# A recurrence's job order, one bias product, one tile's index scores and a closing norm

## The chip, the cores and the metric

One core of a Trainium2 chip runs the whole program in one launch. The metric is the time of an execution on the device in microseconds.

## The reference

Two blocks in a row over 512 tokens of 1024 features. The first has a gated recurrence (RG-LRU) layer and an attention layer that selects its keys, each with an MLP behind it; the second a gated linear attention with a pooling branch and a gated feed-forward layer; a norm closes. The change touches the recurrence, the index scores and the closing norm:

```python
def rglru_mixer(h, w_in, conv_w, conv_b, w_a, b_a, w_x, b_x, lam, w_out):
    gate, xr = jnp.split(h @ w_in, 2, axis=-1)
    gate = jax.nn.gelu(gate)
    xc = conv_b + sum(xpad[:, k:k + S] * conv_w[k] for k in range(4))
    r = sigmoid(blockwise(xc, w_a) + b_a)      # 4 blocks of 256 features
    i = sigmoid(blockwise(xc, w_x) + b_x)
    log_a = -8.0 * r * softplus(-lam)
    a, u = exp(log_a), sqrt(-expm1(2.0 * log_a)) * (i * xc)
    hs = scan(h_t = a_t * h_(t-1) + u_t)
    return (hs * gate) @ w_out

# attention, per block of 128 queries: 8 index heads choose the keys
dots = relu(einsum('bqhd,bsd->bqhs', qi_b, ki))
score = einsum('bqh,bqhs->bqs', wi_b, dots)
_, idx = lax.top_k(where(causal, score, -inf), topk)
logits = einsum('bqhc,bqkc->bqhk', q_lat_b, c_sel) + rel_bias[t5_bucket(dist)]

# at the very end
out = x * rsqrt(mean(x * x, axis=-1) + 1e-6) * norm_final
```

## The kernel before

Activations are kept transposed, as tiles of 128 features by 512 tokens. A matrix product takes its fp32 operands as a high and a low part and sums three matmuls, high by high, high by low and low by high (L349 to L351 in `group`); `lin` (L353) makes one output tile of 1024 inputs with 24 of them. There are eight PSUM banks.

Weights come as chunks of 128x1024 in the order of a table that `weight_plan` (L100) writes. `Weights` (L218) loads a chunk by SP (L246), makes its high part on ACT (L252) and its low part on DVE, or on POOL for the attention's inputs and a few others (L253); buffers of the high and low parts are reused in turn, so a copy waits until PE has left an earlier chunk.

Work is written as jobs, lists of stages. `run` (L269) interleaves them: at each step the next job's first stage, then later stages of the jobs before it. A scheduler of the framework sets the final order on each engine from that, and `tc.high_priority` brings some evictions forward.

In the recurrence `conv_job(j)` makes tile j of `xr` (PE), scales it (DVE, L536), and applies the convolution, one instruction on ACT (L541) and three taps on DVE (L544); `split` copies the high part on ACT (L362) and subtracts the low part on DVE (L363). `recur_job(b)`, called ax below, multiplies two such tiles by the two gates' weights: 24 matmuls into four banks. Tanh on ACT (L568, L569) frees these banks; then exponentials, a square root and factors follow, and a scan on DVE (L598). `rgate_job(j)` makes tile j of `gate`, with a gelu on ACT (L612) and the product with the scan's result on DVE (L615), and splits it: Y. `bias_job` loads two small tables, multiplies them (L635), copies the result on DVE (L639) and stores it to DRAM (L640) for attention. `rout` (L655) is the output product: its first four tiles take all of Y in pairs of tiles.

The order there is written by the loop at L645: xr0 to xr5, ax0, xr6, xr7, ax1, gates 0 and 1, ax2, bias job, gates 2 and 3, ax3, gates 4 to 7.

`index_job(i, h)` (L769) makes the scores of query block i and index head h: two matmuls into a bank (L779), relu with a scale on ACT (L784), then the weighted add into `score`, by ACT for head 0 (L790) and by DVE for the others (L793); for block 3 POOL does three heads. `select` (L802) then takes the largest keys in 16 rounds of two DVE instructions (L811, L812).

The end: `last_job` makes the last down products, four tiles of all tokens, then four tiles of the left 256 tokens, then of the right; each adds to x (L1453), squares (L1427, L1429) and prepares `fin`. `norm_job` (L1460) sums the squares over features with a matrix of ones (L1467), takes the root (L1471) and reciprocal (L1472) of the 128x256 result, in which all 128 rows are alike, multiplies four `fin` tiles (L1477) and stores them (L1478). The left half's norm is put between the right half's jobs.

Of the kernel before, what the change touches and what calls it, by code (L numbers as in the profile page):

```python
# [15 lines left out]
AF = mybir.ActivationFunctionType  # L16
# [80 lines left out]
    return plan  # L97


def weight_plan():  # L100

    plan = []
    for step in range(8):
        plan += [("xr" if step < 4 else "rgate", 2 * step % 8 + i) for i in range(2)]
        if 2 <= step <= 5:
            plan += [("ax", step - 2)]
    plan += [("routk", kk) for kk in range(4)] + [("rout", j) for j in range(4, 8)]
    plan += mlp_plan(0, HID_GROUPS, False)
    plan += [("att", j) for j in (0, 1, 2, 3, 4, 6, 7, 8, 9, 5, 10, 11, 12, 13)] + [("uk",), ("uv",)]
    plan += [("wo", j) for j in range(8)]  # L110
    plan += mlp_plan(1, HID_GROUPS, False)
    plan += [("lr",), ("k", 0), ("k", 1), ("k", 2), ("dec",), ("k", 3)] + [("q", j) for j in range(4)]
    plan += [("u", j) for j in range(4)] + [("v", half, kk) for half in range(2) for kk in range(4)] + [("pg",)]
    plan += [("gb", j) for j in range(8)]
    plan += [("ga", j) for j in range(4)] + [("r", j) for j in range(8)] + [("ga", j) for j in range(4, 8)]
    plan += [("bg", j) for j in range(8)] + [("wo2", j) for j in range(8)]
    plan += mlp_plan(0, HID2_GROUPS, True)
    return plan
# [150 lines left out]
def run(jobs):  # L269

    deep = max(len(j) for j in jobs)
    for step in range(len(jobs) + deep - 1):
        for stage in [0] + list(range(deep - 1, 0, -1)):
            i = step - stage
            if 0 <= i < len(jobs) and stage < len(jobs[i]):
                jobs[i][stage]()
# [3 lines left out]
def build(ctx, tc, xT, wall, par, relb, onehot, edges, out):  # L280
# [12 lines left out]
    def T(dt=F32, name="t"):  # L293
        return tp.tile([P, S], dt, name=name, tag="t")
# [117 lines left out]
    def residual_job(j, mm, feed, half=False):  # L412
        st = {}

        def first():
            st["ps"] = mm()

        def second():
            if half:
                stt(xs[j], st["ps"], 0.5, xs[j], op0=ALU.mult, op1=ALU.add)  # L420
            else:
                V.tensor_add(xs[j], xs[j], st["ps"])  # L422
            if feed is not None:
                feed.add(xs[j])

        return [first, second]
# [124 lines left out]
    def recur_job(b):  # L551
        st = {}

        def mm():
            h, l = W.get("ax", b)
            for nt in range(2):
                for m in range(2):
                    ps = st[nt, m] = PS()
                    o = m * 512 + nt * P
                    group(ps, [(h[:, o + k * 256:o + k * 256 + P], l[:, o + k * 256:o + k * 256 + P], *xcs[2 * b + k])  # L560
                               for k in range(2)])

        def gates():
            for nt in range(2):
                j = 2 * b + nt
                rg, ig = T(name="rg"), T(name="ig")
                with tc.high_priority(offset=EARLY):
                    act(rg, st[nt, 0], AF.Tanh, scale=0.5, bias=hb[:, j:j + 1])  # L568
                    act(ig, st[nt, 1], AF.Tanh, scale=0.5, bias=hb[:, KD + j:KD + j + 1])  # L569
                st[nt] = rg, ig  # L570
            for nt in range(2):
                j = 2 * b + nt
                rg, ig = st[nt]
                q = T(name="q")
                act(q, rg, AF.Exp, scale=nsp[:, j:j + 1], bias=nsp[:, j:j + 1])
                act(q, q, AF.Identity, scale=0.5, bias=half_t)
                act(rg, rg, AF.Tanh, scale=nsp2[:, j:j + 1], bias=nsp2[:, j:j + 1])
                st[nt] = rg, ig, q

        def factors():  # L580
            for nt in range(2):
                rg, ig, q = st[nt]
                stt(ig, ig, 1.0, xc[2 * b + nt], op0=ALU.add, op1=ALU.mult)
                w = T(name="w")
                stt(w, rg, 1.0, q, op0=ALU.subtract, op1=ALU.mult)
                stt(q, w, 2.0, q, op0=ALU.add, op1=ALU.mult)
                V.tensor_mul(ig, ig, q)
            for nt in range(2):
                rg, ig, q = st[nt]
                act(rg, rg, AF.Sqrt, scale=-1.0)  # L590

        def scan():
            for nt in range(2):
                rg, ig, q = st[nt]
                V.tensor_mul(ig, ig, rg)
                act(q, q, AF.Identity, scale=2.0, bias=minus_t)
                hh = hs[2 * b + nt] = T(name="hs")
                V.tensor_tensor_scan(hh, q, ig, 0.0, op0=ALU.mult, op1=ALU.add)  # L598

        return [mm, gates, factors, lambda: None, scan]  # L600
# [24 lines left out]
    def bias_job():  # L625
        st = {}

        def load():
            st["rb"], st["oh"] = T(name="relb"), T(name="oh")
            nc.sync.dma_start(st["rb"][:32, :P], relb)  # L630
            nc.sync.dma_start(st["oh"][:32, :DIST_PITCH], onehot)

        def mm():
            st["ps"] = PS("bias")
            PE.matmul(st["ps"][:, :DIST_PITCH], st["rb"][:32, :P], st["oh"][:32, :DIST_PITCH], start=True, stop=True)  # L635

        def store():
            t = T(name="biasrow")
            V.tensor_copy(t[:16, :DIST_PITCH], st["ps"][:16, :DIST_PITCH])  # L639
            nc.sync.dma_start(bdram, t[:16, :DIST_PITCH])  # L640

        return [load, lambda: None, mm, store]

    jobs = [[lambda: None, softplus]]
    for step in range(8):  # L645
        jobs += [(conv_job if step < 4 else rgate_job)(2 * step % 8 + i) for i in range(2)]
        if 2 <= step <= 5:
            jobs.append(recur_job(step - 2))
        if step == 4:
            jobs.append(bias_job())  # L650
    run(jobs)
    nxt = Feed("g_mlp0")
    rout_ps = []
# [14 lines left out]
                        PE.matmul(rout_ps[i], l[:, c], yh, start=False, stop=kt == KD - 1)  # L668
        return rout_ps[j] if j < 4 else lin(Y, "rout", j)

    run([residual_job(j, lambda j=j: rout(j), nxt) for j in range(KD)])
    feed, nxt = nxt, Feed("g_mix1")
    mlp(0, feed, nxt)

# [95 lines left out]
    def index_job(i, h):  # L770

        st = {}
        w = (i + 1) * P
        on_pool = i == 3 and h in (2, 4, 6)

        def mm():
            ps = st["ps"] = PS("idx")
            for n in range(2):
                PE.matmul(ps[:, :w], qi[h][:, i * P:(i + 1) * P], ki[n][:, :w], start=n == 0, stop=n == 1)  # L779

        def relu():

            d = st["d"] = T(name="dots") if on_pool else st["ps"]
            act(d[:, :w], st["ps"][:, :w], AF.Relu, scale=wis[i][0][:, h:h + 1])  # L784

        def add():
            d, sg = st["d"], wis[i][1][:, h:h + 1]
            if h == 0:
                accs[i] = T(name="score")
                act(accs[i][:, :w], d[:, :w], AF.Copy, scale=sg)  # L790
            else:
                if not on_pool:
                    stt(accs[i][:, :w], d[:, :w], sg, accs[i][:, :w], op0=ALU.mult, op1=ALU.add)  # L793
                else:
                    G.tensor_scalar(d[:, :w], d[:, :w], sg, 1.0, op0=ALU.mult, op1=ALU.mult)
                    G.tensor_add(accs[i][:, :w], accs[i][:, :w], d[:, :w])
            if h == 7:
                V.tensor_add(accs[i][:, w - P:w], accs[i][:, w - P:w], tri)
                ready[i] = True

        return [mm, relu, add]
# [658 lines left out]
    def norm_job(c):  # L1460
        st = {}
        w = c.stop - c.start

        def tot():
            ps = st["ps"] = PS("tot")[:, :w]
            for i in range(2):
                PE.matmul(ps, ones, acc2[i][:, c], start=i == 0, stop=i == 1)  # L1467

        def rstd():
            r = st["r"] = T(name="std")[:, :w]  # L1470
            act(r, st["ps"], AF.Sqrt, scale=1.0 / D, bias=eps_t)  # L1471
            V.reciprocal(r, r)  # L1472

        def outs(pairs):
            for i in pairs:
                z = fin[i, c.start].rearrange("p (d c) -> p d c", d=2)
                V.tensor_mul(z, z, st["r"].unsqueeze(1).to_broadcast([P, 2, w]))  # L1477
                nc.sync.dma_start(out[2 * i:2 * i + 2, :, c].rearrange("d p c -> p d c"), z)  # L1478

        return [tot, rstd, lambda: outs((1, 0)), lambda: outs((2, 3))]  # L1480
# [30 lines left out]
    jobs += [last_job(d, left, first, n, hid) for d in range(KD - 4, KD)]  # L1511
    jobs += [last_job(d, right, first, n, hid) for d in range(KD - 4, KD)]
    norm_left, norm_right = norm_job(left), norm_job(right)
    jobs.insert(-2, norm_left[:3])
    run(jobs)
    norm_right[0]()
    norm_left[3]()
# [32 lines left out]
```

## Time and profile before

| | us |
|---|---|
| median of 3 runs | 1905.28 |
| the runs | 1903.79, 1905.28, 1905.71 |
| profiled execution | 1903.61 |
| its span, first to last instruction | 1901.8 |
| PE, DVE, ACT, POOL busy | 1848.7, 1020.3, 813.4, 181.7 |

Mean granted clock of PE over the span is 0.988 of full speed. Times of the trace count from the start of the span.

### The profile page before, as it was taken

How to read it: one execution, taken by the hardware profiler on the slowest of the kernel's cores; microseconds unless marked ns; L12 is line 12 of the kernel's file. 1: busy time of each engine (PE TensorE's matmuls, PEld its weight loads, DVE VectorE, ACT ScalarE, POOL GpSimd, SP SyncE). 2: the span in 40 equal slices, each digit the busy share in tenths (PEclk: the TensorE clock that was granted, in tenths of full speed). 3: DMA queues.
4: the chain of work that ended last, by engine and by line, in shares of the span. 5: the costliest groups of instructions: out<-in, count | busy, mean ns of one | idle time of the engine just before them, and what ended most of it. 6: DMA issues, size and time to landing. Idle time of an engine off the chain costs nothing.

```text
span 1901.8 us, 21845 instructions
## 1 busy us (share of the span) xinstructions
PE 1848.7 (97%) x8434; PEld 1526.0 (80%) x8434; DVE 1020.3 (54%) x1512; ACT 813.4 (43%) x1271; POOL 181.7 (10%) x194
## 2 busy tenths in 40 slices
PE   8989999999999679999999999999999999999997
PEld 6868888888878468888888888888888888888886
DVE  7886543344349956654244445735584554344345
ACT  6784432333244577443234445446543333132223
POOL 0000000000155264000000014211000000000000
PEclk9999999999999899999999999999999999999998
DMA  5222222222222530322222222231122222222221
GB/s 197 84 86 92 100 98 91 100 100 96 93 100 90 146 89 21 111 93 96 100 100 92 97 100 86 92 111 45 67 89 100 100 89 100 100 95 94 100 80 53
DMA packets 61000, 179.36 MB, mean 94 GB/s; under 512 B 7696, under 2 KB 18144, under 8 KB 60896
## 3 DMA queue, kind: packets, MB, share of 16 engines
q1 hardware_dynamic: 60752, 177.97, 27.6%
q8 instruction: 66, 1.08, 0.2%
q14 instruction: 38, 0.31, 0.0%
q10 hardware_dynamic: 144, 0.00, 0.0%
HBM read 168.48 MB, written 2.12 MB: 90 GB/s over the span
## 4 chain that ended last, share of the span: by engine, by line
PE 63%; DVE 4%; ACT 2%; issue 1%; DMA 0%; POOL 0%; SPq 0%; DVEq 0%; ACTq 0%
PE ps L349 14%; PE ps L351 13%; PE ps L350 13%; PE dn L350 5%; PE dn L351 5%; PE dn L349 5%; PE o L1319 1%; DVE score L812 1%; PE v L1225 1%; PE v L1224 1%; PE v L1226 1%; DVE top L811 1%; ACT probs L941 1%; PE kv L1293 1%; PE tot L376 0%
## 5 line engine op out<-in xcount | busy, mean ns | idle before, releaser
L252 ACT ACTIVATE wh<-wst 128x1024 fp32r<-128x1024 f32 (+2 forms) x314 | 328.2, 1047 | 910.3 <-PE ps L350 358.7
L349 PE MATMUL ps<-xh,wh 128*128 128x512 f32 x1376 | 542.5, 394 | 6.4 <-DVE biasrow L639 4.6
L351 PE MATMUL ps<-xh,wl 128*128 128x512 f32 x1376 | 536.6, 390 | 0.0
L350 PE MATMUL ps<-xl,wh 128*128 128x512 f32 x1376 | 536.5, 390 | 0.0
L253 DVE TENSOR_TENSOR wl<-wst,wh 128x1024 fp32r<-128x1024 f32 (+2 forms) x291 | 352.4, 1212 | 224.3 <-ACT wh L252 197.2
L349 PEld LDWEIGHTS ps<-xh,wh 128*128 128x128 f32 x1376 | 259.3, 188 | 62.8 <-issue 7.2
L350 PEld LDWEIGHTS ps<-xl,wh 128*128 128x128 f32 x1376 | 259.3, 188 | 56.3 <-issue 2.4
L351 PEld LDWEIGHTS ps<-xh,wl 128*128 128x128 f32 x1376 | 259.1, 188 | 54.1
L349 PE MATMUL dn<-h,wh 128*128 128x512 f32 (+1 forms) x712 | 271.7, 382 | 0.0
L350 PE MATMUL dn<-l,wh 128*128 128x512 f32 (+1 forms) x712 | 271.7, 382 | 0.0
L351 PE MATMUL dn<-h,wl 128*128 128x512 f32 (+1 forms) x712 | 271.7, 382 | 0.0
L350 PEld LDWEIGHTS dn<-l,wh 128*128 128x128 f32 x712 | 133.8, 188 | 26.0
L349 PEld LDWEIGHTS dn<-h,wh 128*128 128x128 f32 x712 | 133.8, 188 | 26.0
L351 PEld LDWEIGHTS dn<-h,wl 128*128 128x128 f32 x712 | 133.8, 188 | 25.8
L253 POOL TENSOR_TENSOR wl<-wst,wh 128x1024 fp32r<-128x1024 f32 x23 | 55.2, 2405 | 934.7 <-ACT wh L252 934.5
L422 DVE TENSOR_TENSOR x<-x,dn 128x512 f32<-128x512 f32 x48 | 33.0, 687 | 170.8 <-PE dn L351 170.8
L453 DVE SCALAR_TENSOR_TENSOR relu<-ps,std 128x512 f32<-128x512 f32 x64 | 44.2, 691 | 146.7 <-PE ps L351 146.6
L349 PE MATMUL ps<-h,wh 128*128 128x512 f32 x200 | 78.7, 396 | 5.5 <-ACT h L362 3.5
L350 PE MATMUL ps<-l,wh 128*128 128x512 f32 x200 | 77.8, 389 | 0.0
L351 PE MATMUL ps<-h,wl 128*128 128x512 f32 x200 | 77.8, 389 | 0.0
L349 PEld LDWEIGHTS ps<-h,wh 128*128 128x128 f32 x200 | 37.9, 190 | 15.1 <-ACT h L362 4.0
L1497 DVE TENSOR_TENSOR u<-ps,std 128x512 f32<-128x512 f32 x22 | 15.2, 690 | 62.5 <-PE ps L351 62.5
(315 smaller groups left out, 2129.2 us busy)
## 6 DMA issues: line engine op xcount, KB each, us to landing
wst<-wall SPq DMA_DIRECT2D x300, 512.0 KB, 3.2
btile<-biasdram SPq DMA_DIRECT2D x32, 128.0 KB, 3.0
qd<-qq SPq DMA_DIRECT2D x64, 64.0 KB, 2.1
wst<-wall SPq DMA_DIRECT2D x8, 384.0 KB, 3.0
x<-xT SPq DMA_DIRECT2D x8, 256.0 KB, 4.9
out_dram<-fin SPq DMA_DIRECT2D x8, 256.0 KB, 2.3
wst<-wall SPq DMA_DIRECT2D x6, 256.0 KB, 5.0
kto<-kth SPq DMA_DIRECT2D x8, 128.0 KB, 2.7
```

What stands on the lines that cost most here:

```text
L252: self.nc.scalar.activation(h[:, a:b], st[:, a:b], AF.Copy)
L253: eng.tensor_sub(l[:, a:b], st[:, a:b], h[:, a:b].bitcast(F32))
L349: PE.matmul(ps, wh, xh, start=i == 0, stop=False)
L350: PE.matmul(ps, wh, xl, start=False, stop=False)
L351: PE.matmul(ps, wl, xh, start=False, stop=i == n - 1)
L422: V.tensor_add(xs[j], xs[j], st["ps"])
L453: stt(t, st["ps"], 0.0, feed.r, op0=ALU.max, op1=ALU.mult)
L811: V.max(top, acc[:, :w])
L812: V.match_replace(acc[:, :w], top, acc[:, :w], MARK)
L941: act(s[:, :w], s[:, :w], AF.Exp, scale=-1.0, bias=nm, accum_out=sums[:, a:a + 1])
L1224: PE.matmul(st["ps"][i], xh, hk, start=kt == 0, stop=False)
L1225: PE.matmul(st["ps"][i], xh, lk, start=False, stop=False)
```

## The change

1. The order of the recurrence's jobs becomes a table, LAYER0, that sets jobs and weights alike: xr0 to xr6, ax0, xr7, gate 0, ax1, gates 1 and 2, ax2, gates 3 and 4, ax3, gates 5 to 7.
2. The bias job leaves the recurrence and runs between the fourth and the fifth job of the output product.
3. For query block 1, relu writes its result to a tile in SBUF, not back into its bank. The other blocks stay.
4. The closing norm sums squares with x's columns as weights and a single column of ones, so that 256 tokens become 128x2 numbers with tokens on partitions; root and reciprocal work on 128x2; two products with the identity bring the result back to all rows of 128x256, in a bank that the outputs read. The left half's norm is put one job earlier.

```diff
--- before.py
+++ after.py
@@ -97,13 +97,14 @@
     return plan
 
 
+
+LAYER0 = ([("xr", j) for j in range(7)] + [("ax", 0), ("xr", 7), ("rgate", 0), ("ax", 1), ("rgate", 1), ("rgate", 2)]
+          + [("ax", 2), ("rgate", 3), ("rgate", 4), ("ax", 3)] + [("rgate", j) for j in range(5, 8)])
+
+
 def weight_plan():
 
-    plan = []
-    for step in range(8):
-        plan += [("xr" if step < 4 else "rgate", 2 * step % 8 + i) for i in range(2)]
-        if 2 <= step <= 5:
-            plan += [("ax", step - 2)]
+    plan = list(LAYER0)
     plan += [("routk", kk) for kk in range(4)] + [("rout", j) for j in range(4, 8)]
     plan += mlp_plan(0, HID_GROUPS, False)
     plan += [("att", j) for j in (0, 1, 2, 3, 4, 6, 7, 8, 9, 5, 10, 11, 12, 13)] + [("uk",), ("uv",)]
@@ -642,12 +643,7 @@
         return [load, lambda: None, mm, store]
 
     jobs = [[lambda: None, softplus]]
-    for step in range(8):
-        jobs += [(conv_job if step < 4 else rgate_job)(2 * step % 8 + i) for i in range(2)]
-        if 2 <= step <= 5:
-            jobs.append(recur_job(step - 2))
-        if step == 4:
-            jobs.append(bias_job())
+    jobs += [{"xr": conv_job, "ax": recur_job, "rgate": rgate_job}[n](j) for n, j in LAYER0]
     run(jobs)
     nxt = Feed("g_mlp0")
     rout_ps = []
@@ -668,7 +664,8 @@
                         PE.matmul(rout_ps[i], l[:, c], yh, start=False, stop=kt == KD - 1)
         return rout_ps[j] if j < 4 else lin(Y, "rout", j)
 
-    run([residual_job(j, lambda j=j: rout(j), nxt) for j in range(KD)])
+    jobs = [residual_job(j, lambda j=j: rout(j), nxt) for j in range(KD)]
+    run(jobs[:4] + [bias_job()] + jobs[4:])
     feed, nxt = nxt, Feed("g_mix1")
     mlp(0, feed, nxt)
 
@@ -780,7 +777,7 @@
 
         def relu():
 
-            d = st["d"] = T(name="dots") if on_pool else st["ps"]
+            d = st["d"] = T(name="dots") if on_pool or i == 1 else st["ps"]
             act(d[:, :w], st["ps"][:, :w], AF.Relu, scale=wis[i][0][:, h:h + 1])
 
         def add():
@@ -1462,14 +1459,20 @@
         w = c.stop - c.start
 
         def tot():
-            ps = st["ps"] = PS("tot")[:, :w]
-            for i in range(2):
-                PE.matmul(ps, ones, acc2[i][:, c], start=i == 0, stop=i == 1)
+
+            ps = st["ps"] = PS("tot")
+            for n in range(w // P):
+                cols = slice(c.start + n * P, c.start + (n + 1) * P)
+                for i in range(2):
+                    PE.matmul(ps[:, n:n + 1], acc2[i][:, cols], ones[:, 0:1], start=i == 0, stop=i == 1)
 
         def rstd():
-            r = st["r"] = T(name="std")[:, :w]
-            act(r, st["ps"], AF.Sqrt, scale=1.0 / D, bias=eps_t)
-            V.reciprocal(r, r)
+            col = small(w // P, "rstd")
+            act(col, st["ps"][:, :w // P], AF.Sqrt, scale=1.0 / D, bias=eps_t)
+            V.reciprocal(col, col)
+            st["r"] = PS("r")[:, :w]
+            for n in range(w // P):
+                PE.matmul(st["r"][:, n * P:(n + 1) * P], col[:, n:n + 1].to_broadcast([P, P]), ident, start=True, stop=True)
 
         def outs(pairs):
             for i in pairs:
@@ -1511,7 +1514,7 @@
     jobs += [last_job(d, left, first, n, hid) for d in range(KD - 4, KD)]
     jobs += [last_job(d, right, first, n, hid) for d in range(KD - 4, KD)]
     norm_left, norm_right = norm_job(left), norm_job(right)
-    jobs.insert(-2, norm_left[:3])
+    jobs.insert(-3, norm_left[:3])
     run(jobs)
     norm_right[0]()
     norm_left[3]()
```

In these rows the numbers behind a tile's name tell apart the tiles of one name. PE, at ax0 (h_460 is the high part of the first convolution's tile, xh the layer's input). Before:

```order
L349 MATMUL ps_435<-xh_188,wh_308 128x512
L350 MATMUL ps_435<-xl_189,wh_308 128x512
L351 MATMUL ps_435<-xh_188,wl_309 128x512
L349 MATMUL ps_485<-h_460,wh_340 128x512
L349 MATMUL ps_492<-h_460,wh_340 128x512
L349 MATMUL ps_499<-h_460,wh_340 128x512
```

PE, the end of xr6 and what follows it, now:

```order
L351 MATMUL ps_485<-xl_183,wh_340 128x512
L352 MATMUL ps_485<-xh_182,wl_341 128x512
L350 MATMUL ps_485<-xh_188,wh_340 128x512
L351 MATMUL ps_485<-xl_189,wh_340 128x512
L352 MATMUL ps_485<-xh_188,wl_341 128x512
L350 MATMUL ps_527<-h_460,wh_382 128x512
L350 MATMUL ps_534<-h_460,wh_382 128x512
```

The 24 matmuls of xr6 (ps_485, the last of them shown) now stand ahead of ax0's first ones, which stood right behind xr5 (ps_435).

ACT, ahead of the second ax job's first tanh. Before (h_709 is the high part of xr6's convolution, whose taps are xc_663; xc_713 is xr7's):

```order
L541 ACTIVATE xc_663<-xr_627,params_74 128x512
L252 ACTIVATE wh_735<-wst_734 128x1024
L596 ACTIVATE q_576<-q_576,minus_115 128x512
L362 ACTIVATE h_709<-xc_663 128x512
L541 ACTIVATE xc_713<-xr_668,params_74 128x512
L568 ACT_TABLE_LOAD
L568 ACTIVATE rg_718<-ps_635,half_b_218 128x512
L569 ACTIVATE ig_719<-ps_642,half_b_218 128x512
```

ACT, ahead of the second ax job's first tanh, now (xc_705 and h_752 are xr7's, gate_710 gate 0's):

```order
L542 ACTIVATE xc_705<-xr_669,params_74 128x512
L613 ACT_TABLE_LOAD
L613 ACTIVATE gate_710<-gate_710 128x512
L253 ACTIVATE wh_824<-wst_823 128x1024
L597 ACTIVATE q_614<-q_614,minus_115 128x512
L597 ACTIVATE q_618<-q_618,minus_115 128x512
L363 ACTIVATE h_752<-xc_705 128x512
L569 ACTIVATE rg_757<-ps_677,half_b_218 128x512
L570 ACTIVATE ig_758<-ps_684,half_b_218 128x512
```

The first gelu, with its table load, and the copy of the last convolution now stand ahead of ax1's tanh.

DVE, from the last left product's square to the end. Before:

```order
L1433 TENSOR_TENSOR sq<-sq 128x256
L1472 RECIPROCAL std<-std 128x256
L1453 TENSOR_TENSOR x<-x,dn 128x256
L1477 TENSOR_TENSOR fin<-fin,std 128x512 x4
L1433 TENSOR_TENSOR sq<-sq 128x256
L1453 TENSOR_TENSOR x<-x,dn 128x256
L1429 TENSOR_TENSOR sq<-x 128x256
L1472 RECIPROCAL std<-std 128x256
L1477 TENSOR_TENSOR fin<-fin,std 128x512 x4
```

DVE, the same place, now (r is the bank with the two identity products):

```order
L1430 TENSOR_TENSOR sq<-sq 128x256
L1472 RECIPROCAL rstd<-rstd 128x2
L1450 TENSOR_TENSOR x<-x,dn 128x256
L1480 TENSOR_TENSOR fin<-fin,r 128x512 x4
L1430 TENSOR_TENSOR sq<-sq 128x256
L1450 TENSOR_TENSOR x<-x,dn 128x256
L1430 TENSOR_TENSOR sq<-sq 128x256
L1450 TENSOR_TENSOR x<-x,dn 128x256
L1426 TENSOR_TENSOR sq<-x 128x256
L1472 RECIPROCAL rstd<-rstd 128x2
L1480 TENSOR_TENSOR fin<-fin,r 128x512 x4
```

The left half's reciprocal and outputs moved from behind the right half's second square to behind its first, and the reciprocals are of 128x2.

## Rows read from the trace of the kernel before

**Rows 1.** The page: busy time, share of the span and instructions of each engine.
```profile
PE 1848.7 (97%) x8434; PEld 1526.0 (80%) x8434; DVE 1020.3 (54%) x1512; ACT 813.4 (43%) x1271; POOL 181.7 (10%) x194
```

**Rows 2.** Timeline, PE: start, us, engine, line, operation, tiles, count [idle before, releaser].
```profile
40.99 0.39 PE L350 MATMUL ps<-xl,wh 128*128 128x512 f32 x1
41.21 0.39 PE L351 MATMUL ps<-xh,wl 128*128 128x512 f32 x1
45.15 1.22 PE L349 MATMUL ps<-h,wh 128*128 128x512 f32 x2 [3.54 <-ACT h L362]
...
120.42 0.77 PE L349 MATMUL ps<-xh,wh 128*128 128x512 f32 x1 [4.61 <-DVE biasrow L639]
...
123.12 0.50 PE L349 MATMUL ps<-xh,wh 128*128 128x512 f32 x1
```

**Rows 3.** Busy time by stretch: length, each engine (instructions), PEclk, DMA share, GB/s.
```profile
41.44:131.97 90.53, 80.41 (x336) 64.58 (x336) 76.81 (x105) 74.64 (x100) 0.00 (x0) 0.96 0.22 78
60.00:80.00 20.00, 20.00 (x90) 16.57 (x89) 17.56 (x24) 15.60 (x22) 0.00 (x0) 1.00 0.32 113
80.00:100.00 20.00, 18.59 (x79) 14.07 (x77) 17.58 (x25) 19.91 (x28) 0.00 (x0) 1.00 0.29 101
120.00:122.00 2.00, 1.58 (x4) 1.32 (x5) 2.00 (x4) 1.08 (x2) 0.00 (x0) 0.50 0.05 12
```

**Rows 4.** Waits of PE, 20 to 140 us: total, times, longest.
```profile
PE ps L349 <- DVE biasrow L639: 4.6, 1, 4.6
PE ps L349 <- ACT h L362: 3.5, 1, 3.5
PE ps L349 <- ACT rg L568: 2.0, 2, 1.1
```

**Rows 5.** Timeline, ACT, before the first tanh.
```profile
58.71 1.28 ACT L568 ACT_TABLE_LOAD   x1
```

**Rows 6.** Timeline at the index scores: PE, DVE, POOL; two subtractions on DVE.
```profile
563.02 0.50 PE L349 MATMUL ps<-xh,wh 128*128 128x512 f32 x1 [1.77 <-ACT score L790]
...
563.00 3.74 DVE L793 SCALAR_TENSOR_TENSOR score<-idx,sg,score 128x256 f32<-128x256 f32 x7 [3.25 <-ACT score L790]
...
558.66 4.70 POOL L253 TENSOR_TENSOR wl<-wst,wh 128x1024 fp32r<-128x1024 f32 x2
...
600.25 2.40 POOL L253 TENSOR_TENSOR wl<-wst,wh 128x1024 fp32r<-128x1024 f32 x1 [7.33 <-ACT wh L252]
...
600.73 2.48 DVE L363 TENSOR_TENSOR l<-c,h 128x512 fp32r<-128x512 f32 x1 [0.36 <-ACT h L362]
...
52.22 0.69 DVE L363 TENSOR_TENSOR l<-xc,h 128x512 fp32r<-128x512 f32 x1 [0.76 <-ACT h L362]
```

**Rows 7.** Timeline of the end; then two groups by form (busy us, mean ns).
```profile
1888.54 0.28 PE L351 MATMUL dn<-h,wl 128*128 128x256 f32 x1
1891.60 2.08 PE L1467 MATMUL tot<-sq,ones 128*128 128x256 f32 x4 [2.78 <-DVE sq L1433]
...
1888.73 2.48 DVE L1477 TENSOR_TENSOR fin<-fin,std 128x512 f32<-128x512 f32 x4
...
1891.47 0.41 DVE L1453 TENSOR_TENSOR x<-x,dn 128x256 f32<-128x256 f32 x1
...
1894.22 1.75 DVE L1472 RECIPROCAL std<-std 128x256 f32<-128x256 f32 x1 [1.88 <-ACT std L1471]
1896.01 2.50 DVE L1477 TENSOR_TENSOR fin<-fin,std 128x512 f32<-128x512 f32 x4
...
1893.71 0.47 ACT L1471 ACTIVATE std<-tot,eps 128x256 f32<-128x256 f32 x1 [1.30 <-PE tot L1467]
...
1892.39 0.56 PEld L1467 LDWEIGHTS tot<-sq,ones 128*128 128x128 f32 x2 [0.29 <-DVE sq L1429]
...
L943 DVE RECIPROCAL sums<-sums 128x2 f32<-128x2 f32 x32 | 5.1, 160 | 9.6 <-ACT probs L941 9.6
...
L736 PE MATMUL wiT<-ident,kw 128*128 128x128 f32 x3 | 0.5, 272 | 0.0
```

## The prediction

> **What bounds the kernel now.** I read the page first, then PE's waits, then busy time by stretches, then the timeline of each engine at the four places that the change touches. PE works 97% of the span [rows 1], so the time is PE's work plus PE's idle time, and an edit pays only where it takes idle time or a lower clock from PE, or where it shortens the chain behind PE's last product. None of the four parts takes products away.
>
> In the recurrence PE issues a 128x512 matmul every 0.227 us (40.99 and 41.21 are two in a row of them [rows 2]), so the 24 of one job take 5.44 us. The stretch from the end of the sixth convolution job to just short of the output product is 90.53 us long and holds 336 matmuls [rows 3]: 336 x 0.227 = 76.2 us, and 0.9 us for the bias product. About 13.5 us are lost. The reader is to see in the waits [rows 4] that 10.1 of them are idle: 4.6 for the copy of the bias row, 3.5 for a convolution's copy (ax0 needs the first one), 2.0 for the first tanh of an ax job, which frees a bank. The other 3.4 are matmuls at the lower of the two clock levels: after the idle 4.61 us the granted clock is 0.50 (1.2 GHz) [rows 3], and the first six matmuls take 120.42 to 123.12, 2.70 us where 1.36 would do [rows 2].
>
> **Part 1, the new order; part 2, the bias later.** *ax0's wait.* PE reaches ax0 one job (5.44 us) later than now and waits 3.54 us now [rows 2]; what it waits for, taps on DVE, is not behind anything new. The wait goes, with its lower clock.
>
> *ax1.* PE ends xr6, ax0, xr7 and rgate0 at 41.44 + 4 x 5.44 = 63.2. The weight copy that stands on ACT ahead of ax0's tanh needs the weight buffer that PE leaves there. Then come four ACT instructions, one a table load of 1.28 [rows 5]; at ACT's mean of 0.711 us (19.91 over 28 [rows 3]) for the other three, tanh starts at 66.6 and frees a bank at 67.3. PE wants it for ax1's third product at 63.2 + 12 x 0.227 = 65.9: a wait of 1.4.
>
> *ax2.* PE is there after the wait, half of ax1, two gate jobs and half of ax2: 65.9 + 1.4 + 16.3 = 83.6. It waits for ax1's first tanh, 23 ACT instructions after ax0's. If ACT never waits that is 23 x 0.711 = 16.4 after 66.6, so 83.0, and free at 83.7: a wait of 0.1, the lower end. But just ahead of that tanh now stands the copy of the last convolution, for which DVE must first have done its three taps. DVE's step before that run is the low part of xc_6, whose high part is the 12th ACT instruction, done at 66.6 + 12 x 0.711 = 75.1; then follow 17 DVE instructions, weight splits, factors and a scan between the taps, at 17.56 / 24 = 0.73 us [rows 3] 12.4 us, to 87.5; with copy and tanh the bank is free at 88.9: a wait of 5.3, the upper end. I take 4.6, near the upper end, since the DVE run has no gap in which to catch up.
>
> *ax3.* PE is there at 83.6 + 4.6 + 16.3 = 104.5. Ax1's first tanh began at 88.2 - 0.7 = 87.5; ax2's stands 24 ACT instructions, 17.1 us, behind it, and frees the bank at 105.3: a wait of 0.8 if ACT never waits; if it waits as in the list before (87.5 - 66.6 - 16.4 = 4.5) 5.3. I take 1.2, nearer the lower end: this list has no taps left in it.
>
> Waits then are 1.4 + 4.6 + 1.2 = 7.2 for 10.1. Waits of 1.1 us and less are not followed by a lower clock now (1.00 in 80 to 100 [rows 3]); the one of 4.6 should be, once, for half of today's 3.4. The recurrence gains 2.9 + 1.7 = **4.6 us**; by the ends it lies between a gain of 11 (waits 1.4, 0.1, 0.8, no lower clock) and a loss of 2 (1.4, 5.3, 5.3, two stretches of lower clock).
>
> The extra table load (a tanh after a gelu in the first list) is ACT's 1.28 and is inside the count above. The bias product itself is only moved (0.9 us on either side). Its two loads and its store go to SP's queue past some weight loads; SP issues them in the output-product stage, where the weights come as in the rest, and the DVE copy there has nothing queued behind it that PE needs soon, since each output job covers 5.44 us. The bias is read some 450 us later. Nothing.
>
> **Part 3, index scores of one tile.** Now each relu writes into its PSUM bank, so a bank stays taken until DVE has added it; PE loses 1.77 us there, before 563.02 [rows 6], and DVE adds the seven scores in 3.74 us from 563.00 [rows 6]. With the copy in SBUF the bank is free after the relu, and PE goes on about 1.8 us sooner. But both operands of DVE's adds are now in SBUF, and POOL splits weights until 558.66 + 4.70 = 563.36 [rows 6]. What that can do shows at 600.73: a subtraction of 128x512, 0.69 us elsewhere, takes 2.48, as long as POOL's split from 600.25 [rows 6]. So the adds gain nothing before 563.36, or hold POOL up. The Trainium skill, page "SBUF — State Buffer", section "Who interferes with whom", says that a DVE instruction with two SBUF inputs excludes a GpSimd instruction that reads SBUF, the later one blocking fully, while one SBUF input does not: it speaks against this part. The trace agrees, 2.48 for 0.69. What follows is top-k selection, which is DVE's, and attention after it waits for DVE, POOL and ACT, so PE's 1.8 would be waited for later. I take 0; ends: a gain of 1.8, and a loss of 2.4, one POOL split that DVE has to sit out.
>
> **Part 4, the closing norm.** PE's last down matmul begins at 1888.54 [rows 7], but x is added only at 1891.47, since DVE is on the left half's reciprocal and outputs (2.48). Moved one job earlier with a small reciprocal, those are done in time, and x follows the last product. PE gets more work ahead of it: eight weight loads for the one-column sums instead of four, two products with the identity. At 0.28 per load at the lower clock (0.56 for two) and 0.27 for a 128-column record [rows 7] I put 1.1 us on PE: x is added at 1890.0, a gain of 1.4. From that add to the first output is 1896.01 - 1891.47 = 4.54 now. Of it go a reciprocal of 1.75 (128x2 takes 0.16 [rows 7]) and about 0.2 of the root's 0.47 (128x2 for 128x256); what comes is two identity products with their hop, 0.6 to 0.8; the sums stay as long (six loads at 0.28 after the last square, against 2.08 for four passes now). That is 1.75 - 0.16 + 0.2 - 0.7 = 1.1. The four outputs stay at 2.50. Together **2.5 us**; ends 1.0 (the sums are twice as long, PE is held by the root) and 4.0.
>
> **Sum.** 4.6 + 0 + 2.5 = 7.1 us. Against the profiled execution, 1903.61, that is 1896.5. It lies 1.7 under the median of the runs, 1905.28, so I forecast 1905.28 - 7.1 = **1898.2**. A measurement can tell about 0.2%, 3.8 us, from no change.
>
> **Rivals.**
> *B, the whole loss goes.* If DVE catches up before the last convolution's taps, ax2 waits under 1 us and no lower clock follows: 1.4 + 0.9 + 0.8 = 3.1 lost for 13.5, a gain of 10.4, with the closing 12.9: 1892.4; halfway to it, 1895. For: ACT alone would be ready at 83.7. Against: DVE is at 17.6 of 20 us from 60 to 100 [rows 3].
> *C, the wait only moves.* ACT's second list waits for DVE as its first does: ax3 waits 5.3 and a second stretch of lower clock follows, 4.1 + 1.7 = 5.8 worse: 1904.0. For: ACT is at 19.91 of 20 us in 80 to 100. Against: no taps left.
> *D, slower.* ACT's and DVE's queue is late by the same 4.5 us once more when PE comes to the output product, which now has only three gate jobs behind ax3 where four stand now. PE starts it on the first gated tiles and needs the last two 3 x 5.44 = 16.3 us later; from the point at which the last tile is later than that, PE waits again: 4.5 and 1.7 of lower clock on top of C, 1910.2. Against: today no wait stands there at all [rows 4].
> *E, part 3 costs its upper end*, 2.4: 1900.6. By the page's rule this is what DVE's two-SBUF adds would do if POOL's split comes first each time.
>
> **How the numbers follow.** Forecast 0.60, B 0.18, C 0.12, D 0.04, E 0.06. The forecast's own range, from the ends of the closing and of ax2, is 1895 to 1901.5. The range 1892.5 to 1903.5 takes in B nearly whole and E, and leaves out C's middle and D. Faster by over 3.8 us, below 1901.5: nearly all of the forecast (0.58), B, most of E (0.04): 0.80. Within: C, the rest of the forecast and of E: 0.16. Slower by over 3.8 us: D, 0.04.
>
> **What would show it.** PE's waits from 20 to 140: no bias row, no convolution copy, but an ax job's tanh with three waits, the middle one 3 to 5 us, and one stretch of granted clock near half. If that middle wait is short, B; if the third is as long, C; if one stands at the output product, D. At 560: no 1.8 us wait of PE, the seven adds over by about 567 as now. At the end: x added within 0.3 us of the last down product, about 3.4 us from there to the first output. The prediction is wrong if a wait appears where none is named, or if the gain of the recurrence is handed back in attention.

## The result, and the profile after

The changed kernel takes 1890.98 us (median of 4 runs, 1890.31 to 1891.35) against 1904.53 before: the ratio is 0.9928, with an interval from 0.9911 to 0.9945. It is 13.5 us faster where 7.1 were forecast, and lies below the range. The profiled execution took 1890.85, its span is 1889.0.

First the page's busy time, then PE's waits from 20 to 160 us:

```profile
PE 1846.3 (98%) x8449; PEld 1526.4 (81%) x8450; DVE 1018.5 (54%) x1512; ACT 814.0 (43%) x1272; POOL 182.2 (10%) x194
```
```profile
PE ps L350 <- ACT rg L569: 5.4, 2, 4.0
```

PE's share rose from 97 [rows 1] to 98%. Of the three waits [rows 4] the one for the bias row and the one for a convolution's copy are gone; the tanh's stands twice as before, now for 5.4 us where it was 2.0. The timeline of PE shows where, the table by stretch what follows:

```profile
66.24 0.50 PE L350 MATMUL ps<-h,wh 128*128 128x512 f32 x1 [1.43 <-ACT rg L569]
...
86.89 0.80 PE L350 MATMUL ps<-h,wh 128*128 128x512 f32 x1 [3.99 <-ACT rg L569]
87.48 0.63 PE L351 MATMUL ps<-l,wh 128*128 128x512 f32 x1
...
91.22 0.39 PE L350 MATMUL ps<-xh,wh 128*128 128x512 f32 x1
...
104.83 0.40 PE L350 MATMUL ps<-h,wh 128*128 128x512 f32 x1
```
```profile
88.00:90.00 2.00, 2.00 (x6) 1.56 (x5) 1.15 (x2) 1.97 (x3) 0.00 (x0) 0.50 0.00 0
90.00:92.00 2.00, 2.00 (x10) 1.61 (x9) 0.04 (x1) 2.00 (x4) 0.00 (x0) 0.98 0.00 0
```

66.24 is the first matmul for ax1's third bank, 86.89 for ax2's, 104.83 for ax3's: waits of 1.43, 3.99 and none. After the middle one the granted clock is 0.50 (1.2 GHz) in 88 to 90, and 0.98 in 90 to 92. The second half of ax2, 12 matmuls, takes from 86.89 to 91.22, 4.33 us for 12 x 0.227 = 2.72, so the lower clock costs 1.6. Why ax2 waits stands on DVE and ACT:

```profile
73.46 0.69 DVE L364 TENSOR_TENSOR l<-xc,h 128x512 fp32r<-128x512 f32 x1 [0.61 <-ACT h L363]
...
79.41 0.75 DVE L545 SCALAR_TENSOR_TENSOR xc<-xr,params,xc 128x509 f32<-128x509 f32 x1
...
81.27 0.74 DVE L545 SCALAR_TENSOR_TENSOR xc<-xr,params,xc 128x510 f32<-128x510 f32 x1
...
83.67 1.22 DVE L599 TENSOR_TENSOR_SCAN hs<-q,ig 128x512 f32<-128x512 f32 x1
84.81 0.73 DVE L545 SCALAR_TENSOR_TENSOR xc<-xr,params,xc 128x511 f32<-128x511 f32 x1
```
```profile
81.58 1.32 ACT L597 ACTIVATE q<-q,minus 128x512 f32<-128x512 f32 x2
85.63 0.63 ACT L363 ACTIVATE h<-xc 128x512 fp32r<-128x512 f32 x1 [2.73 <-DVE xc L545]
86.16 0.67 ACT L569 ACTIVATE rg<-ps,half_b 128x512 f32<-128x512 f32 x1
...
104.00 0.67 ACT L569 ACTIVATE rg<-ps,half_b 128x512 f32<-128x512 f32 x1
```

DVE works without a gap from xc_6's low part (73.46) to xr7's third tap (to 85.54); ACT waits 2.73 us for it with the copy at 85.63, and the tanh stands behind that. The next ax job's first tanh is at 104.00.

The index scores, on DVE and POOL, and the adds by operands (min, median and max in ns):

```profile
553.89 5.55 DVE L790 SCALAR_TENSOR_TENSOR score<-dots,sg,score 128x256 f32<-128x256 f32 x7 [1.97 <-ACT dots L781]
559.54 0.29 DVE L795 TENSOR_TENSOR score<-score,tri 128x128 f32<-128x128 f32 x1
```
```profile
550.52 5.10 POOL L254 TENSOR_TENSOR wl<-wst,wh 128x1024 fp32r<-128x1024 f32 x2
```
```profile
L790 DVE SCALAR_TENSOR_TENSOR score<-dots,sg,score x7: 484/484/2015, 553.9 to 559.0; 128x256 f32<-128x256 f32 x7
```

Seven adds take 5.55 us for 3.74 [rows 6]: six take 0.48, one takes 2.02 while POOL's split runs. PE has no wait there any more; it had 1.77 [rows 6].

The end, on PE, DVE and ACT:

```profile
1879.29 0.28 PE L352 MATMUL dn<-h,wl 128*128 128x256 f32 x1
1879.41 0.38 PE L1467 MATMUL tot<-ones,sq 128*128 128x1 f32 x2
1880.55 0.83 PE L1467 MATMUL tot<-ones,sq 128*128 128x1 f32 x6 [0.76 <-DVE sq L1426]
1881.93 1.12 PE L1475 MATMUL r<-ident,rstd 128*128 128x128 f32 x4 [0.55 <-DVE rstd L1472]
```
```profile
1879.61 0.42 DVE L1450 TENSOR_TENSOR x<-x,dn 128x256 f32<-128x256 f32 x1 [0.26 <-PE dn L352]
1880.07 0.42 DVE L1426 TENSOR_TENSOR sq<-x 128x256 f32<-128x256 f32 x1
1881.70 0.17 DVE L1472 RECIPROCAL rstd<-rstd 128x2 f32<-128x2 f32 x1 [1.22 <-ACT rstd L1471]
1883.08 2.48 DVE L1480 TENSOR_TENSOR fin<-fin,r 128x512 f32<-128x512 f32 x4 [1.21 <-PE r L1475]
```
```profile
1881.41 0.26 ACT L1471 ACTIVATE rstd<-tot,eps 128x2 f32<-128x2 f32 x1 [0.84 <-PE tot L1467]
```

x is added 0.04 us after the last down product ends, not after the outputs of the other half [rows 7], and from there to the first output it is 1883.08 - 1879.61 = 3.47 us, where it was 4.54.

To compare kernels I use marks of each profiled execution, in us: the starts of the first product, of the output product, of the first index score, of attention's last transpose of probabilities (last pT) and of the linear attention's first kv product, and the span.

| kernel | first product | output product | first score | last pT | kv | span |
|---|---|---|---|---|---|---|
| before | 7.7 | 132.8 | 558.9 | 744.1 | 1286.3 | 1901.8 |
| changed | 6.4 | 123.9 | 551.0 | 734.0 | 1276.2 | 1889.0 |
| changed, again (e9) | 7.3 | 124.9 | 552.0 | 734.3 | 1276.5 | 1888.8 |
| order alone (e1) | 6.7 | 131.7 | 557.7 | 742.5 | 1284.8 | 1900.3 |
| bias later alone (e5) | 6.8 | 125.8 | 554.7 | 737.7 | 1279.9 | 1895.1 |
| order and bias (e7) | 6.2 | 125.1 | 552.3 | 736.8 | 1279.0 | 1894.4 |
| scores alone (e2) | 7.2 | 134.4 | 560.4 | 742.5 | 1284.7 | 1900.1 |
| changed less scores (e3) | 7.4 | 124.9 | 552.1 | 735.0 | 1277.2 | 1889.5 |
| the same again (e14) | 6.5 | 125.9 | 553.1 | 738.1 | 1280.4 | 1892.7 |
| closing alone (e4) | 6.2 | 132.6 | 558.6 | 743.9 | 1286.2 | 1898.9 |
| head 0 alone (e6) | 7.4 | 125.0 | 552.1 | 734.1 | 1276.3 | 1888.6 |
| copy later (e12) | 7.6 | 122.7 | 549.8 | 731.4 | 1273.6 | 1885.9 |
| gate early (e10) | 6.3 | 121.3 | 555.7 | 737.7 | 1279.9 | 1892.2 |
| xr7 first (e11) | 6.4 | 120.8 | 559.4 | 740.3 | 1282.6 | 1894.9 |
| e10, bias later still (e15) | 7.3 | 120.2 | 548.8 | 731.1 | 1273.3 | 1885.6 |
| e11, bias later still (e16) | 6.6 | 121.3 | 550.2 | 732.2 | 1274.5 | 1886.8 |
| e12, head 0 alone (e17) | 7.5 | 122.6 | 549.7 | 732.9 | 1275.1 | 1887.9 |

Where did the 13.5 us come from? Up to the first score, the mean of before, e2 and e4, which share a recurrence, is 559.3, and of the changed one, e3, e6, e7, e9 and e14 552.1: 7.2 us. From the first score to the last pT, the seven kernels without the scores by SBUF take 182.9 to 185.3, mean 184.4; the ten others (two of them with head 0 alone) take 180.9 to 183.2, mean 182.1: 2.3 us. From kv to the end it is 615.5 before and 612.3 to 612.8 in all with the new closing: 3.0 us. Together 12.5, within the measured interval (10.5 to 17).

### The profile page after: what moved, and what is told of

It reads as the page before. It is cut to its first block, busy times and chain, and to the rows that moved or that the text cites. A ratio compares the mean times of both kernels' runs of the same rounds, so it can differ in the third digit from the quotient of the medians.

```text
span 1889.0 us, 21879 instructions
## 1 busy us (share of the span) xinstructions
PE 1846.3 (98%) x8449; PEld 1526.4 (81%) x8450; DVE 1018.5 (54%) x1512; ACT 814.0 (43%) x1272; POOL 182.2 (10%) x194
## 4 chain that ended last, share of the span: by engine, by line
PE 90%; DVE 6%; ACT 3%; issue 1%; DMA 0%; POOL 0%; DVEq 0%; ACTq 0%; SPq 0%; POOLq 0%
PE ps L350 19%; PE ps L351 19%; PE ps L352 19%; PE dn L351 8%; PE dn L352 8%; PE dn L350 8%; DVE score L809 1%; DVE top L808 1%; PE o L1316 1%; PE ps L521 1%; ACT probs L938 1%; PE v L1221 1%; PE v L1223 1%; PE v L1222 1%; DVE score L790 1%
## 5 line engine op out<-in xcount | busy, mean ns | idle before, releaser
L350 PEld LDWEIGHTS ps<-h,wh 128*128 128x128 f32 x200 | 37.9, 190 | 14.7 <-ACT rg L569 6.4
```

The lines of the kernel that those rows point to most:

```text
L350: PE.matmul(ps, wh, xh, start=i == 0, stop=False)
```

## The experiments

**The parts by themselves.** The order alone (e1), that is the change with the bias job put back behind ax2:

```diff
-    jobs = [residual_job(j, lambda j=j: rout(j), nxt) for j in range(KD)]
-    run(jobs[:4] + [bias_job()] + jobs[4:])
+    run([residual_job(j, lambda j=j: rout(j), nxt) for j in range(KD)])
...
+    jobs.insert(2 + LAYER0.index(("ax", 2)), bias_job())
```

with scores and closing as before. Expected:

> The new job order alone; the bias product stays right behind ax2, scores and closing norm as before. If the order alone gives the recurrence's gain: PE's waits for a convolution copy and, mostly, the lower clock behind it go (3.5 + 2.0), but the wait for the bias row on DVE stays (3 to 5 us): 3 to 5 us faster, 1900 to 1902. If order and late bias only work together, the wait for the bias row grows by what the other saves: within 1 us of before.

Measured: 1903.25, ratio 0.9996 (0.9987 to 1.0006). Its waits of PE from 20 to 160:

```profile
PE ps L350 <- ACT rg L569: 5.4, 2, 4.0
PE ps L350 <- DVE biasrow L640: 4.2, 1, 4.2
```

They sum to 9.6, for 10.1 before [rows 4]: the order alone only exchanges the wait for the copy for waits on the tanh. The 3 to 5 us of the first reading did not come; the second reading has the time, but not for its reason, since the wait for the bias row did not grow (4.2 for 4.6).

The bias product later, alone (e5): in the kernel before, the job is put between the output jobs as in the change, and

```diff
-        if step == 4:
-            jobs.append(bias_job())
```

> The bias product later, in the old order. If the wait for the bias row was a wait of its own, it goes with the lower clock behind it: 5 to 7 us faster, 1897 to 1899, and PE waits 5.5 us between 20 and 140. If the gate tiles behind ax3 only come to wait for another thing on ACT or DVE there, the wait moves: within 2 us of before. In both cases the new order's own worth is the changed kernel's recurrence less this.

Measured: 1897.01, ratio 0.9966 (0.9953 to 0.9978): 6.7 us faster, as by the first reading, with waits of 6.4 us:

```profile
PE ps L349 <- ACT h L362: 3.9, 1, 3.9
PE ps L349 <- ACT rg L568: 1.7, 2, 0.9
PE ps L351 <- DVE wl L253: 0.8, 1, 0.8
```

Order and bias together (e7), that is the change less these:

```diff
-            d = st["d"] = T(name="dots") if on_pool or i == 1 else st["ps"]
+            d = st["d"] = T(name="dots") if on_pool else st["ps"]
...
-    jobs.insert(-3, norm_left[:3])
+    jobs.insert(-2, norm_left[:3])
```

and `norm_job` as before.

> New order and late bias, scores and closing norm as before. If the parts add up: from the first product to the output product 117.5 us (117.5 in the changed kernel, 125.1 to 127.2 in four kernels that lack one of the two), and 8 to 9 us faster than before, 1895 to 1896. If it needs the scores or the closing norm too: over 1898.

Measured: 1894.57, ratio 0.9952 (0.9939 to 0.9966), 9.2 us under its own before; the first score comes at 552.3, as in the changed kernel. From the first product to the output product it took 118.9, not 117.5: the first began at 6.2, but the output product no sooner than in e3, e6 and e9 (125.1 for 124.9 to 125.0). So the late bias brings most of the recurrence's gain. On top of it the order brings 2.4 us more by the medians (1897.01 and 1894.57), where alone it brought nothing; the intervals of e5 and e7 overlap, so these 2.4 are likely and not shown.

The scores by SBUF alone (e2), one line in the kernel before:

```diff
-            d = st["d"] = T(name="dots") if on_pool else st["ps"]
+            d = st["d"] = T(name="dots") if on_pool or i == 1 else st["ps"]
```

> One tile's scores by SBUF alone. Theory 1 (PE's own wait counts): PE's 1.8 us and the lower clock behind it go, and 2 to 3 us are left at the end although DVE's seven adds take 5.5 instead of 3.7: about 1902. Theory 2 (selection on DVE sets the time, as I predicted): the adds end later, 0 to 1 us slower.

Measured: 1900.93, ratio 0.9986 (0.9977 to 0.9996): faster by about 3 us, by theory 1. The changed kernel less that line (e3), and again (e14):

> The changed kernel without the scores by SBUF. Theory 1: 2 to 3 us slower than the changed kernel, 1893 to 1894. Theory 2 (the 2.2 us that attention gained came from the shift of phases that the new order brings): as the changed kernel, 1891.

> The changed kernel without the scores by SBUF, again, beside the changed kernel's own five rounds. If the part is worth what it gave alone (2.6 us), 1893 to 1894; if most of PE's gain there is waited for later in attention, 1891 to 1892.

Measured: 1891.74 and 1892.85, ratios 0.9941 (0.9926 to 0.9956) and 0.9941 (0.9929 to 0.9954), against 0.9928 and 0.9931 (e9) for the changed kernel. These intervals overlap, so alone they don't settle it; the seventeen profiled executions of the table, taken by part, put it at 2.3 us, with a small overlap of the two groups.

The closing norm alone (e4), `norm_job` of the change in the kernel before, and

```diff
-    jobs.insert(-2, norm_left[:3])
+    jobs.insert(-3, norm_left[:3])
```

> The closing norm alone. If the parts add up: 2.6 us faster, 1902, with x added within 0.3 us of the last down product. Also a look at the start: the first product began at 7.7 us before and at 6.4 in the changed kernel; if that is chance, it begins at either in these four runs whatever the recurrence's order; if the order causes it, it begins at 6.4 in those with the new order and 7.7 in the others.

Measured: 1901.41, ratio 0.9987 (0.9977 to 0.9996), 2.7 us faster. The start is chance: 6.2 here with the old order, 7.4 in e3 with the new one.

The changed kernel once more (e9):

> The changed kernel once more, for the comparison on the same chip and a second look at chance: 1891, recurrence 117.5 us with waits of 1.4 and 4.0; the start of the first product may differ by up to 1.5 us and the stretches of lower clock in attention may lie elsewhere.

Measured: 1890.72, ratio 0.9931 (0.9919 to 0.9944), the same two waits.

**What blocks DVE's adds.** Only head 0 of the tile by SBUF (e6):

```diff
-            d = st["d"] = T(name="dots") if on_pool or i == 1 else st["ps"]
+            d = st["d"] = T(name="dots") if on_pool or (i == 1 and h == 0) else st["ps"]
```

> The changed kernel with only head 0 of that tile by SBUF, the other seven in place as before. PE's bank is then free early, and DVE's adds keep one operand in PSUM. If POOL's split blocks adds with both operands in SBUF: the seven adds take 3.7 us again, selection starts about 1.8 us sooner after the first score product than in the changed kernel. If the blocking had another cause: 5.5 as in the changed kernel. The time: 0 to 2 us under the changed kernel.

Measured: 1890.55, ratio 0.9929 (0.9917 to 0.9942). DVE's timeline, and POOL's:

```profile
556.31 3.15 DVE L790 SCALAR_TENSOR_TENSOR score<-idx,sg,score 128x256 f32<-128x256 f32 x6 [3.29 <-ACT score L787]
...
560.64 0.47 DVE L790 SCALAR_TENSOR_TENSOR score<-idx,sg,score 128x256 f32<-128x256 f32 x1
561.22 2.33 DVE L795 TENSOR_TENSOR score<-score,tri 128x128 f32<-128x128 f32 x1
563.58 0.43 DVE L808 MAX8 top<-score 128x8 f32<-128x256 f32 x1
```
```profile
551.60 5.09 POOL L254 TENSOR_TENSOR wl<-wst,wh 128x1024 fp32r<-128x1024 f32 x2
560.99 2.41 POOL L254 TENSOR_TENSOR wl<-wst,wh 128x1024 fp32r<-128x1024 f32 x1 [4.30 <-ACT wh L253]
```

With the dots in PSUM the adds take 0.47 to 0.53 each. But now the triangle's add, whose operands are both in SBUF, starts at 561.22 inside POOL's next split and takes 2.33 us for 0.29. So an instruction with both operands in SBUF is held beside POOL's split, whichever instruction meets it. One with an operand in PSUM is not, as the changed kernel shows for the next query block, whose dots stay in PSUM; this add lies inside a split, and takes no longer than its neighbours (0.60 and 0.61):

```profile
568.22 0.60 DVE L790 SCALAR_TENSOR_TENSOR score<-idx,sg,score 128x384 f32<-128x384 f32 x1
```
```profile
566.78 2.41 POOL L254 TENSOR_TENSOR wl<-wst,wh 128x1024 fp32r<-128x1024 f32 x1 [4.47 <-ACT wh L253]
```

The adds of e6 start later, behind the first head's on ACT (3.29), so selection starts at 563.58, where it is 560.83 in e9 with the first score at the same 552. I had expected 1.8 us sooner. These 2.7 us don't show in the time (1890.55 and 1890.72). PE's wait for a bank is gone here too, with one head by SBUF. The Trainium skill, page "SBUF — State Buffer", section "Who interferes with whom", has this rule, for two SBUF inputs and for at most one, and both kernels agree with both halves of it (2.33 us for 0.29; 0.60 for 0.60).

**What sets the wait at ax2.** The last convolution's split one step later (e12):

```diff
-        return [mm] + [lambda: None] * max(0, 2 - j) + [evict, taps, out_]
+        return [mm] + [lambda: None] * max(0, 2 - j) + [evict, taps] + [lambda: None] * (j == 7) + [out_]
```

> The changed kernel with the split of the last convolution (its copy on ACT, its subtraction on DVE) one step later, so that the copy stands behind ax1's tanh on ACT, not ahead of it. If the 4.0 us wait at ax2 is the taps of xr7 that this copy waits for: ACT is free for the tanh at 82.9 instead of 86.2, the wait falls to about 0.7, the lower clock behind it goes (1.6), ax3 may wait up to 1.5 since PE comes sooner: 3 to 5 us under the changed kernel, 1886 to 1888. If ACT's own list sets it (as rival C has it): the wait stays at 3 to 4, or stands at ax3: 1890 to 1891.

Measured: 1887.98, ratio 0.9913 (0.9899 to 0.9926), about 3 us under the changed kernel. PE's timeline:

```profile
84.71 0.50 PE L350 MATMUL ps<-h,wh 128*128 128x512 f32 x1 [0.63 <-ACT rg L569]
...
103.49 0.50 PE L350 MATMUL ps<-h,wh 128*128 128x512 f32 x1 [2.16 <-ACT rg L569]
```

The wait at ax2 is 0.63, the lower clock is gone, and ax3, which PE now reaches sooner, waits 2.16, where 1.5 at most had been expected. The output product starts at 122.7, 2.2 us before e9's.

**How much more.** One gate job more ahead of ax1 to ax3 (e10), and xr7 ahead of ax0 as well (e11); of the order only e10's new line is shown:

```diff
+    "xr0 xr1 xr2 xr3 xr4 xr5 xr6 ax0 xr7 rgate0 rgate1 ax1 rgate2 rgate3 ax2 rgate4 rgate5 ax3 rgate6 rgate7").split()]
...
-        return [mm, gelu, prod, out_]
+        return [mm, gelu, lambda: None, prod, out_]
```

> The changed kernel with one gate job more ahead of ax1, ax2 and ax3, two behind ax3 (a gate's product is a step later, as its order needs). If PE's waits are only a question of how early it comes: it comes to ax1 5.4 us later than its bank is free, all three waits go, and with them 5.4 + 1.6 us: 1884 to 1886, unless the output product then waits for the last two tiles. If ACT and DVE set the stretch's length (rival D): the wait stands at the output product, 1889 to 1893.

> As the run before, with xr7 ahead of ax0 as well, so that PE comes to ax0 10.9 us later than in the kernel before, and all ax jobs stand together with two gate jobs between. By the first reading as the run before or 0 to 1 us better; by the second the chain from ax3 to the output product is 5.4 us later still and PE waits 3 to 6 us there: 1891 to 1895.

Measured: 1894.05 and 1896.39, ratios 0.9947 (0.9933 to 0.996) and 0.996 (0.9946 to 0.9973), both slower than the changed kernel. Neither reading was right. In e10 the output product starts at 121.3, 2.6 us sooner than in the changed kernel, and the first score at 555.7, 4.7 later. The waits of e10 from 20 to 180, and SP's from 100 to 165:

```profile
PE bias L636 <- DMA oh<-onehot: 4.3, 1, 4.3
PE ps L350 <- ACT rg L569: 2.5, 2, 1.8
```
```profile
SPq L247 <- DVE wl L254: 52.5, 10, 8.3
```
```profile
154.62 0.42 SPq L632 DMA_DIRECT2D oh<-onehot  x1
```

The bias product waits 4.3 us for its table: the load is issued at 154.62 only, behind weight loads in SP's queue that wait for DVE to free their buffers. In the changed kernel it goes out at 149.72, lands 2.8 us later and is needed at 156.6, 4 us on. So with the bias job two output jobs later (e15; e16 the same from e11):

```diff
-    run(jobs[:4] + [bias_job()] + jobs[4:])
+    run(jobs[:6] + [bias_job()] + jobs[6:])
```

> The kernel with one gate job more ahead of ax1 to ax3, and the bias job two output jobs later (10.9 us). If the 7.3 us that it lost in the output product are the bias product's wait for its table (4.3) and the lower clock behind it: both go, the first score product comes at 548 to 549 instead of 555.7, and the time is 1886 to 1888. If ACT's and DVE's late work sets that stretch (rival D), another wait takes its place: 1892 to 1894.

> The same edit in the kernel with xr7 ahead of ax0, which lost 11.5 us in the output product with a wait of 6.7 for the table. By the first reading the first score product comes at 548 to 549 and the time is 1886 to 1888; by the second 1893 to 1896.

Measured: 1887.45 and 1887.63, ratios 0.9914 (0.9897 to 0.993) and 0.9915 (0.9901 to 0.993). The wait for the table is gone and nothing took its place but 0.9 us for a weight's copy (1.4 in e16, as in e11). The best kernels, e12, e15 and e16, are about 3 us under the changed one, by different ways. Their gains were not tried together.

Last, e12 with only head 0 by SBUF (e17):

> The best kernel so far (the last convolution's copy behind the tanh) with only head 0 of the tile by SBUF. If DVE's blocked adds cost time at the end, 0.5 to 1.5 us under it: 1886.5 to 1887.5; if attention waits for other things, the same: 1888.

Measured: 1889.95, ratio 0.9927 (0.9912 to 0.9942), not faster than e12. The intervals overlap, but its four runs (1889.47 to 1890.34) all lie above e12's five (1886.65 to 1888.54). In the profiled executions the first scores are level (549.7 and 549.8), selection starts 2.5 us later (561.15 for 558.62), the last pT comes 1.5 later, and 0.5 more is lost at the very end. Whether the later selection costs those 1.5 us stays open.

## Why the prediction was wrong in size

The direction was right, and so was the place of the gains in the recurrence and at the end; three terms of the sum were too small, the scores' at 0 among them.

*The recurrence, 4.6 forecast, 7.2 measured.* Ax0's wait went as forecast. Ax1's 1.4 is 1.43. Ax2's 4.6 is 3.99; the run of 17 DVE instructions ahead of it took 12.1 us for 12.4, but began 1.6 us sooner, while PE came 0.7 sooner (82.9 for 83.6). Part of both is that the first product began 1.3 us sooner in this execution. The step that failed is **ax3's 1.2 us: there is no wait.** I put PE there after ax2's wait and three jobs, and counted the lower clock as a loss beside it. But that lower clock falls between the two: it makes PE 1.6 us later at ax3, and so covers its wait. PE came at 104.83; ACT, 24 instructions after 86.16, began its tanh at 104.00, after 17.8 us where I had put 17.1, and the bank was free at 104.67. Without the 1.6 us PE would have come at 103.2 and waited 1.4. e12 shows the reverse: without the lower clock ax3 waits 2.16, of which 0.9 is its longer list on ACT, which now holds the copy (18.8 us from tanh to tanh, 83.99 to 102.77). So 5.4 us of waits remain, not 7.2. That is 4.7 us less than before. The other 2.5 of the 7.2 are lower clock and small losses, forecast at 1.7 from one execution. The loss before was a little larger than the 13.5 I started from, since the 336 matmuls counted there include the two of the bias product (0.45 us). And the lower clock varies: with the same recurrence and nearly the same waits the output product starts at 132.6 to 134.4 in before, e2 and e4, 1.8 us apart. In e14, which has the changed kernel's recurrence and 4.01 us of wait at ax2, the granted clock stays low about twice as long:

```profile
90.00:92.00 2.00, 2.00 (x6) 1.59 (x5) 0.12 (x1) 1.99 (x3) 0.00 (x0) 0.50 0.00 0
92.00:94.00 2.00, 2.00 (x7) 1.51 (x7) 0.69 (x1) 2.00 (x5) 0.00 (x0) 0.62 0.00 0
```

*The scores, 0 forecast, 2.3 measured.* The step that failed is **"PE's 1.8 would be waited for later"**. PE got its 1.8 and, against this execution of before, the lower clock behind it, and came from the first to the last score product in 38.2 us (551.0 to 589.2) for 41.8 (558.9 to 600.7); 1.5 came back between the first logits and the first pT (16.2 us for 14.7), the rest stayed. I had followed selection alone. It starts 8.8 us after the first score (559.87), where it was 8.3 (567.17), so POOL's split did hold DVE (1.8 us in the adds), and no cost of it shows at the end: in e6 selection started 2.7 us later still, in the same time. That a later selection never costs anything is not shown; e17 may be such a case. What PE does between the scores are its own projections, and these it did sooner. Rival E had the mechanism right and the price wrong.

*The closing, 2.5 forecast, 3.0 measured.* From the add to the first output it is 3.47 us for the 3.4 I gave. The add came 1.8 us sooner, seen from kv (603.4 us for 605.2), for 1.4: PE was held for 0.8 us by what stands ahead of its last product, where I had put 1.1. Two errors behind the add nearly cancel, and both go with the clock. I priced the sums by loads of before, 0.28 each, which ran at a granted clock of 0.50, and took them to last as long as then; they ran at 1.00, and from their start to the root it is 0.9 us for 1.3. The identity products took 1.12 for 0.6 to 0.8, since the lower clock fell on them; in e9 it did not, and they took 0.71. In PE's stretches, length, busy time and count, granted clock, DMA share and GB/s: first before, then the changed kernel's sums and identity products, and e9's identity products on its timeline:

```profile
1892.00:1893.00 1.00, 1.00 (x3) 0.50 1.08 383
```
```profile
1880.40:1881.40 1.00, 0.83 (x6) 1.00 0.00 0
1882.40:1883.10 0.70, 0.65 (x4) 0.50 0.00 0
```
```profile
1882.22 0.71 PE L1475 MATMUL r<-ident,rstd 128*128 128x128 f32 x4 [0.55 <-DVE rstd L1472]
```

*Rivals.* B named nearly this time, but by waits of 3.1 us where 5.4 are; e15, with 3.4, comes nearest to it. C (a wait that moves to ax3) fell, for the reason above. D fell: no wait stands at the output product in the changed kernel; but e10 and e11 show a wait there, for a transfer, which I had costed at nothing. That cost was right by a margin of 4 us.

*Where the recurrence's gain sits.* I had put it on the order first. By e1, e5 and e7 it is mostly the late bias (6.7 of 9.2); the order alone is worth nothing measurable.

## What to carry to other kernels

Waits in a row are not added up one by one: move PE by each wait and by each stretch of lower clock before the next is costed, since a loss ahead covers a wait behind it. A small job with a load, a product and a copy is best placed where no engine on the path waits behind any of the three; ask for its load's place in the issuing queue too, for a load behind others that wait for buffers comes late. Size a lower clock from more than one execution.

## What the runs showed of the hardware

The first product starts at 6.2 to 7.7 us in executions of the same opening code, and no relation to the change is seen. The same waits cost PE's clock different amounts: waits of 0.66 and 1.80 us at ax2 and ax3 were followed by a granted clock of 0.51 (108 to 110) in e10 and by 1.00 throughout in e15, and the 1.8 us at the scores by 0.50 (558 to 560) in e7 and by 1.00 throughout in e1 and e3. A 128x128 add on DVE of 0.29 us took 2.33 when it met POOL's split, and a single one of seven adds of 0.48 took 2.02; an add with an operand in PSUM took its usual 0.60 inside such a split. One-column fp32 products are cheap: six records in 0.83 us, right behind 0.76 us of idle PE, at a granted clock of 1.00.
